# Four edits to an encoder layer's order of work: banks for row transposes, earlier weight splits and a reload, the rank of an output group, and the home of one weight block

## The chip, the cores and the metric

The kernel runs on one core of a Trainium2 chip. A core has five engines with queues of their own: PE (TensorE, matmuls and transposes), DVE (VectorE), ACT (ScalarE), POOL (GpSimd) and SP (SyncE, which here only issues DMAs). Each engine takes its instructions in the order in which the program gives them. The metric is the device time of one execution in microseconds (us); a time is the median of several runs.

## What is computed

One layer of an encoder, all in float32, on x of 1024 positions by 1024 channels. Each sub-layer stands between RMS norms and adds to x:

```python
h = rmsnorm(x, g_mix_pre);  proj = h @ w_in
y_fox = forgetting_attention(q, k, v, f_logit)        # 8 heads of 64, causal, with a decay bias
y_chk = chunked_relpos_attention(q, k, v, rel_bias)   # 8 heads of 64, own chunk and 8 before it
y = concatenate([rmsnorm(y_fox, g_fox_out), rmsnorm(y_chk, g_chk_out)])
x = x + rmsnorm(y @ w_out, g_mix_post)
h = rmsnorm(x, g_mem_pre);  mem_n = rmsnorm(mem, g_mem_kv)
x = x + rmsnorm(memory_cross_attention(h, mem_n, w_mq, w_mk, w_mv, w_mo), g_mem_post)   # 4 heads of 256, 256 memory rows
h = rmsnorm(x, g_ff_pre)
x = x + rmsnorm(square(relu(h @ w_ff1)) @ w_ff2, g_ff_post)                             # hidden 4096
```

## The kernel before

**Splits.** Every float32 operand of a large product is split into a high part (`hi`, a rounded copy made by ACT) and a low part (`lo`, the rest, a subtraction on DVE or POOL). A product is then three matmuls (`mm3`, line 191): hi by hi, hi by lo, lo by hi. So each weight block that PE uses has a load on SP, a `hi` on ACT and a `lo` behind it, and each result that PE uses again has a copy on ACT and a subtraction on DVE.

**Buffers.** Large tiles come from shared sets: `u4` (30 buffers of 128 x 1024 values), `klo` (4 buffers for the low parts of the attention keys), `w` (2 pairs for split weights), `wq` (1 pair, second stage only), `wraw` (3 for weights as loaded). Results of PE land in eight banks, two each under the names `mm`, `s`, `tr` and `pv`.

**Three stages.**

1. Projections and attention. Eight pairs of heads follow one another in the order `ORDER` (line 346). Scores (`score_steps`), transposes of the probabilities (`turn_steps`, tile `ptr`) and products with the values (`value_steps`, tile `pv`) run over heads and groups of 256 queries. What lies between them is `filler_steps` (line 1342): the projections, then `memory_steps` (line 908), which makes the memory keys (tile `mk`, 8 blocks) and the memory values (tile `mv`, 8 weight blocks named by half nh and pair kp: mv 00 to mv 13).
2. Output products `mix_steps` (tile `yw`, weights `wo`), in two groups g of heads and two halves th of positions; closing of rows; query products `query_steps` (tile `mq`); memory scores and transposes (`ms`, `mtr`); memory output products (`memory_out_steps`, tile `mo` in the `pv` banks); `product_steps` (tile `ym`).
3. The feed-forward part, in which blocks of the first product are formed with sums of blocks so that seven products do the work of eight.

**The planner.** The order within stages 1 and 2 isn't written out. `Flow` (line 56) plays the work forward on a clock of its own with a cost for each step. Each PE step is a generator's yield: a cost and a condition. `Flow.run` takes, at each point of the planned time, the first stream in its list whose condition holds, and so lays down PE's order. Work of the other engines is put into lists (`put`, `chain`, `load`) with the time from which it may start, a cost and a level; each engine takes the lowest level first, then the earliest. The costs set only this order; on the chip every instruction waits for its real inputs. `Tokens` (line 39) counts free buffers and banks in planned time: a condition such as `free["u4"].ready(4)` holds when four are free.

- `Stock` (line 367) loads and splits the weight blocks in one fixed order. `home` says where the split block goes: `w`, `wq` or two `u4` buffers. The split of a block waits until its home is free, and those behind it wait with it. `done` (line 445) gives the buffers back.
- `memory_steps` asks for four free `u4` buffers and both `mm` banks ahead of the first mv step (line 934).
- `Outputs` (line 962) reads back the attention outputs, seven `u4` buffers for each of four groups, as soon as all scores are done; `one` (line 978) makes `yT_hi`, `yT_lo` and the sum of squares `sq`, all at level 1. The sums over channels (tile `ssh`) are made by `rstd_steps`. Splits of weights stand at level 2 on ACT and level 1 on DVE.
- `close_row` (line 1076) ends a row of 128 positions: a first root (`inverse_rms`, line 1041: two small POOL instructions), the addition to x (line 1087), a square sum on ACT, a second root, and the scaled row (line 1093). The planner's cost of one root is 0.95.
- `row_steps` (line 1156) transposes the scaled rows, four at a time into one bank, for `h2T` (both halves) and `h3T` (first half): 8 groups each. Its yield wants a `tr` bank; ACT copies `hi` (line 1181), DVE subtracts `lo` (line 1178), and then the bank is free.

**The start of the feed-forward part** (lines 1721 to 1835) is written out by hand. Four units (`Turn`, line 1649) transpose the last rows (`turn`, tile `trx`), form sums of blocks with their high parts (`sums`), and make the low parts (`low`). Between them PE works through the first products of seven blocks (`ahead`, line 1626: tiles `px` and `py`, 12 matmuls each), whose weights `split_ahead` (line 1618) splits, `hi` on ACT (line 1579) and `lo` on DVE (line 1582). Their results go to memory and `reload` brings each back for the main loop. Before the change, block 3 is split behind `units[1].low()`, block 5 behind `units[3].sums()`, and the first `reload` is issued behind the load of block 1's second weights.

Of the kernel before, what the change touches and what calls it, by code (L numbers as in the profile page):

```python
# [14 lines left out]
F32 = mybir.dt.float32  # L15
# [7 lines left out]
P = 128  # L23
# [112 lines left out]
def build(ctx, tc, nc, out, t):  # L136
# [230 lines left out]
    class Stock:  # L367
# [3 lines left out]
        def __init__(self):  # L371
            self.blocks = []
            for n, (kind, pr) in enumerate(ORDER):
                if n == 5:
                    self.blocks.append("norm")
                b = (0 if kind == "f" else 8) + pr
                self.blocks.append((("q", n), t["w_qk"][b], [P, KC, P]))
                if n > 3:
                    self.blocks.append((("v", n), t["w_v"][n - 4], [P, KC, P]))
                if n == 7:  # L380
                    self.blocks.append("mem")
                self.blocks.append((("k", n), t["w_qk"][b + 4], [P, KC, P]))
# [12 lines left out]
            self.home.update({("mk", nb): "u4" for nb in range(1, KC, 2)})  # L395
            self.home.update({("mv", nh, kp): "u4" for nh in range(2) for kp in (1, 3)})
            turn = 0
            for b in self.blocks:
                if b[0][0] in ("mq", "mo"):
                    if b[0][:3] == ("mo", 1, 1):  # L400
                        self.home[b[0]] = "u4"
                    elif b[0][:2] != ("mo", 1):
                        self.home[b[0]] = ("w", "w", "wq")[turn % 3]
                        turn += 1
            self.raw, self.w, self.turned = {}, {}, 0
            self.to_load, self.to_split = list(self.blocks), []
# [9 lines left out]
        def hi(self, key):  # L416
            raw, nm = self.raw[key], "_".join(map(str, key))
            home, shape = self.home.get(key, "w"), list(raw.shape)
            if home == "w":
                w = [wp.tile(shape, F32R, tag=x, bufs=2, name=x + nm) for x in ("whi", "wlo")]  # L420
            elif home == "wq":
                w = [p2x.tile(shape, F32R, tag="wq", bufs=2, name=x + nm) for x in ("whi", "wlo")]
            else:
                w = [u4(x + nm, shape) for x in ("whi", "wlo")]
            nc.scalar.activation(w[0], raw, AF.Copy)
            self.w[key] = w
# [17 lines left out]

        def done(self, key):
            home = self.home.get(key, "w")
            for _ in range(1 + (home == "u4")):
                free[home].give(flow.end)

        def pump(self):  # L450

            while self.to_load:
                if isinstance(self.to_load[0], str):
                    n = 3 if self.to_load[0] == "norm" else 2
                    if not free["raw"].ready(n):
                        break
                    for _ in range(n):
                        free["raw"].take()
                    (mem_norm if self.to_load.pop(0) == "norm" else mem_loads)()
                    break  # L460
                if not free["raw"].ready():
                    break
                free["raw"].take()
                key = self.to_load[0][0]
                self.load()
                flow.put("D", flow.now, 0.55, lambda: None, lambda at, k=key: seen.__setitem__(("raw", k), at + 4.2))
            while self.to_split and there(("raw", self.to_split[0])):
                key = self.to_split[0]
                home = self.home.get(key, "w")
                n = 1 + (home == "u4")  # L470
                if not free[home].ready(n):
                    break
                for _ in range(n):
                    free[home].take()
                self.to_split.pop(0)
                vec = key[0] not in "qkv" and (key[0] != "mk" or key[1] % 2)
                self.turned += 1

                def halves(at, key=key, eng="V" if vec else "G"):
# [482 lines left out]
    class Outputs:  # L962
# [15 lines left out]
        def one(self, th, g):  # L978
# [3 lines left out]
            os = [u4(f"oin{th}{g}{i}", (P, 2, HT), F32) for i in range(2)]  # L982
            parts[th, g] = yh, yl, sq
            split = all_of(("y", th, g), 4)

            def summed(at):
                adds = [lambda o=o: nc.vector.tensor_add(sq, sq, o) for o in
# [4 lines left out]
                    for _ in range(2):  # L992
                        free["u4"].give(end)

                flow.chain(at, [("V", 0.7, call) for call in adds], done, 1)

            squared = all_of(("squares", th, g), 4, summed)
            for i in range(2):
                for j in range(2):
# [4 lines left out]
                    def loaded(at, gc=gc, o=o, dh=dh, dl=dl, dst=dst):  # L1004
# [2 lines left out]
                            ("V", 0.75, lambda: nc.vector.scalar_tensor_tensor(  # L1007
                                dl, o, gc, f(dh), op0=ALU.mult, op1=ALU.subtract))],
                            lambda end: (split(end), flow.put("S", end, 0.63, lambda: nc.scalar.activation(
                                dst, o, AF.Square), squared, 1)), 1)  # L1010

                    flow.load(flow.now, lambda o=o, kc=kc: nc.sync.dma_start(o, od[kc][th]), loaded, 7.0 - 3 * g)

# [62 lines left out]
    def close_row(nm, n, at, dst, gnext, then):  # L1076
# [5 lines left out]
        def root(k, a, b=None):  # L1082
            r[k] = inverse_rms(a, f"r{nm}{n}{k}", b)
# [5 lines left out]
        def store(end):  # L1089
            flow.load(end, lambda: nc.sync.dma_start(dst[n], xin[nm, n]), mark(("x1d", n)) if nm == "w" else None, 3)  # L1090
            rest = [("S", 1.1, lambda: square_sum(xin[nm, n], s2)),
                    ("G", 0.95, lambda: root(1, s2)),
                    ("V", 1.3, lambda: nc.vector.scalar_tensor_tensor(y, xin[nm, n], r[1], gains[gnext],
                                                                      op0=ALU.mult, op1=ALU.mult))]
            flow.chain(end, rest, lambda t_: (free["xt"].give(t_), then(t_)), 1)
# [5 lines left out]
            else:  # L1101
                flow.put("G", end + 0.5, 0.0, lambda: None, wait)

        flow.put("G", at, 0.95, lambda: root(0, ss[:, 0:1], ss[:, 1:2]), wait, 1)

    def mix_steps(g):

# [48 lines left out]
    def row_steps(nm, th, dst, name):  # L1156

        for a in (0, 2):
            for k in range(0, KC, 2):
                yield (0.436, lambda: there(*((dst, th * 4 + a + q) for q in range(2))) and free["tr"].ready()  # L1160
                       and ((dst, th) in acts or free["u4"].ready(8)))
                if (dst, th) not in acts:
                    for _ in range(8):
                        free["u4"].take()
                    acts[dst, th] = Act(f"{name}{th}")
                free["tr"].take()
                act, y = acts[dst, th], ys[nm, th][0]
                tr = mm_tile([P, 2, 2, P], f"tr_{name}{th}{a}{k}", "tr")
                for j in range(2):
                    for q in range(2):  # L1170
                        nc.tensor.transpose(tr[:, j, q, :], y[a + q][:, (k + j) * P:(k + j + 1) * P], ident)
# [2 lines left out]
                dh = act.h[i][:, o:o + 2, a * P:a * P + 256]  # L1174
                dl = act.l[i][:, o:o + 2, a * P:a * P + 256]

                def lo(at, src=src, dh=dh, dl=dl, key=(dst, "T", th, a, k)):
                    flow.put("V", at, 0.7, lambda: nc.vector.tensor_sub(dl, src, f(dh)),
                             lambda end: (free["tr"].give(end), seen.__setitem__(key, end)))

                flow.put("S", flow.end, 0.6, lambda src=src, dh=dh: nc.scalar.activation(dh, src, AF.Copy), lo)
        for _ in range(4):
# [570 lines left out]
    pws = [pool("pw0")]  # L1753
    pw = pws[0]
    add[1]()
    units[1].low()
    split_ahead(3, raws.pop(3))
    raws[6] = ff1_raw(6)
    add[2] = ahead(2)
    units[2].turn()  # L1760
# [5 lines left out]
    class Weights:  # L1766
# [27 lines left out]
        def split(self, n):  # L1794
# [4 lines left out]
            else:  # L1799
                self.w[n] = HiLo(raw, width, p, tag, 2, f"{n}{self.j}").both(nc.vector)  # L1800

    cur, nxt = Weights(0), Weights(1)
    cur.load(0)
    cur.load(1)
    nxt.load(0)
    add[3] = ahead(3)
    units[2].low()
    add[3]()
    units[3].turn()
    units[3].sums()  # L1810
    split_ahead(5, raws.pop(5))
    add[4] = ahead(4)
    add[4]()
    units[3].low(1)
# [1 line left out]
    nxt.load(1, True)  # L1816
    cur.sums(nc.vector)
    cur.sum4(nc.vector)
    saved = {}

    def reload(j):
        both = u4(f"p1r{j}", (P, 2, HT), F32)
        nc.sync.dma_start(both, p1d[j])
        saved[j] = both[:, 0, :], both[:, 1, :]

    reload(0)
    add[5] = ahead(5)
    cur.split("s23")
    units[3].low(2)
# [340 lines left out]
```

## Time and profile before

| | us |
|---|---|
| median of 3 runs | 1495.43 |
| lowest and highest | 1493.68, 1496.63 |
| the profiled execution | 1496.05 |
| its span, first to last instruction | 1494.3 |

The profile is of one execution. Its page gives the busy time of each engine, and further views answer questions to the trace: groups of instructions with their mean durations, waits with what ended them, instructions in order of time, and the busy time in chosen stretches with the TensorE clock that was granted. In a row of the timeline the first number is the start in us from the span's start, the second the duration, then engine, line, operation, written tile, read tiles and shape; the bracket at the end is the idle time of the engine just before it and what ended it. PE, PEld, DVE, ACT, POOL and SPq stand for matmuls, weight loads, the three other computing engines and the queue that issues DMAs.

### The profile page before, as it was taken

What the parts mean: (1) busy time and instruction counts of PE and PEld (TensorE: products, weight loads), DVE (VectorE), ACT (ScalarE), POOL (GpSimd) and SP (SyncE); (2) the same over time, 40 slices, a digit from 0 to 9 for tenths busy, and PEclk for the clock granted to TensorE, in tenths of its full rate; (3) what the DMA queues carried; (4) which work ended last, traced back from release to release, by engine and by line L of the source; (5) the groups of instructions that cost most, each with busy time, mean ns of one, the idle gap of its engine ahead of it and who ended that gap; (6) DMA issues with size and microseconds to landing.
All of it is one profiled execution on the core that took longest, in us unless ns stands there. A gap on an engine that the chain in (4) does not pass through costs nothing.

```text
span 1494.3 us, 21605 instructions
## 1 busy us (share of the span) xinstructions
PE 1471.7 (98%) x7606; PEld 1252.0 (84%) x7606; DVE 949.8 (64%) x1644; ACT 798.4 (53%) x1417; POOL 387.5 (26%) x613
## 2 busy tenths in 40 slices
PE   8999999999999999999999999999999999999998
PEld 8989888888889888888888887888888888888886
DVE  6777667566576825974374687674555665646577
ACT  6567577565577735553353455555555553443442
POOL 0144455344345200421031413333233000000021
PEclk9999999999999999999999999999999999999999
DMA  7133222422315642451241446764445695436475
GB/s 269 48 86 80 80 66 84 134 68 58 90 45 167 199 132 85 151 202 57 87 168 57 141 156 202 261 234 155 150 149 180 227 346 195 141 126 212 171 252 197
DMA packets 83485, 220.68 MB, mean 148 GB/s; under 512 B 10008, under 2 KB 14112, under 8 KB 83376
## 3 DMA queue, kind: packets, MB, share of 16 engines
q1 hardware_dynamic: 83376, 219.30, 44.5%
q8 instruction: 60, 0.98, 0.3%
q14 instruction: 49, 0.40, 0.1%
HBM read 159.96 MB, written 50.91 MB: 141 GB/s over the span
## 4 chain that ended last, share of the span: by engine, by line
PE 91%; DVE 4%; ACT 1%; DMA 1%; POOL 1%; issue 1%; SPq 0%; DVEq 0%; POOLq 0%; ACTq 0%
PE ptr L692 4%; PE fx L194 4%; PE fx L195 4%; PE fx L193 4%; PE fy L194 3%; PE fy L193 3%; PE fy L195 3%; PE px L195 3%; PE px L194 3%; PE px L193 3%; PE pv L730 2%; PE pv L729 2%; PE k L193 2%; PE k L194 2%; PE k L195 2%; PE yw L194 2%
## 5 line engine op out<-in xcount | busy, mean ns | idle before, releaser
L698 DVE TENSOR_TENSOR pl<-ptr,ph 128x512 fp32r<-128x512 f32 (+1 forms) x152 | 92.3, 616 | 39.6 <-ACT ph L701 34.6
L1894 ACT ACTIVATE whif<-ra 128x1024 fp32r<-128x1024 f32 x37 | 39.2, 1060 | 120.5 <-PE fy L194 62.6
L1896 DVE TENSOR_TENSOR wlof<-ra,whif 128x1024 fp32r<-128x1024 f32 x37 | 45.3, 1226 | 89.6 <-ACT whif L1894 89.6
L701 ACT ACTIVATE ph<-ptr 128x512 fp32r<-128x512 f32 (+1 forms) x152 | 79.3, 540 | 39.3 <-PE ptr L692 33.2
L2010 POOL TENSOR_SCALAR rf<-sf 128x1 f32<-128x1 f32 x8 | 8.2, 1027 | 326.6 <-ACT jf L1995 326.3
L730 PE MATMUL pv<-pl,vs 128*128 128x256 f32 x304 | 79.3, 285 | 1.9 <-DVE pl L698 1.9
L729 PE MATMUL pv<-ph,vs 128*128 128x256 f32 x304 | 80.1, 287 | 0.0
L193 PE MATMUL fx<-vhif,whif 128*128 128x512 f32 x168 | 65.4, 389 | 0.0
L195 PE MATMUL fx<-vhif,wlof 128*128 128x512 f32 x168 | 65.4, 389 | 0.0
L194 PE MATMUL fx<-vlof,whif 128*128 128x512 f32 x168 | 65.4, 389 | 0.0
L730 PEld LDWEIGHTS pv<-pl,vs 128*128 128x128 f32 x304 | 57.8, 190 | 6.6 <-DVE pl L698 1.5
L729 PEld LDWEIGHTS pv<-ph,vs 128*128 128x128 f32 x304 | 57.5, 189 | 4.0
L1784 POOL TENSOR_TENSOR sc<-wf,wf 128x512 f32<-128x512 f32 x14 | 21.4, 1530 | 145.4 <-DMA wf<-in_w_ff 105.9
L193 PE MATMUL k<-hT_hi,whik 128*128 128x512 f32 x128 | 52.6, 411 | 0.0
L193 PE MATMUL mq<-h2T_hi,whimq 128*128 128x512 f32 x128 | 52.1, 407 | 0.0
L193 PE MATMUL q<-hT_hi,whiq 128*128 128x512 f32 x128 | 50.9, 398 | 0.0
L194 PE MATMUL yw<-wlowo,yT_hi 128*128 128x512 f32 x128 | 49.9, 390 | 0.6 <-DVE wlowo L431 0.6
L193 PE MATMUL ym<-whimo,oT_hi 128*128 128x512 f32 x128 | 50.3, 394 | 0.1
L193 PE MATMUL yw<-whiwo,yT_hi 128*128 128x512 f32 x128 | 50.3, 393 | 0.0
L194 PE MATMUL k<-hT_lo,whik 128*128 128x512 f32 x128 | 50.2, 392 | 0.0
L195 PE MATMUL mq<-h2T_hi,wlomq 128*128 128x512 f32 x128 | 50.1, 392 | 0.0
L194 PE MATMUL q<-hT_lo,whiq 128*128 128x512 f32 x128 | 50.1, 391 | 0.0
(606 smaller groups left out, 5032.5 us busy)
## 6 DMA issues: line engine op xcount, KB each, us to landing
ra<-gd SPq DMA_DIRECT2D x56, 512.0 KB, 3.9
wg<-in_w_ff SPq DMA_DIRECT2D x56, 512.0 KB, 6.2
wf<-in_w_ff SPq DMA_DIRECT2D x38, 512.0 KB, 4.1
gd<-s SPq DMA_DIRECT2D x48, 256.0 KB, 2.1
wrawmq<-in_w_mq SPq DMA_DIRECT2D x16, 512.0 KB, 3.7
wrawmo<-in_w_mo SPq DMA_DIRECT2D x16, 512.0 KB, 3.8
gd<-u SPq DMA_DIRECT2D x32, 256.0 KB, 2.1
gd<-g SPq DMA_DIRECT2D x25, 256.0 KB, 2.4
```

The costliest lines, as they stand in the source:

```text
L193: nc.tensor.matmul(ps, lh, rh, start=start, stop=False, skip_group_check=more)
L194: nc.tensor.matmul(ps, lh, rl, start=False, stop=False, skip_group_check=more)
L195: nc.tensor.matmul(ps, ll, rh, start=False, stop=stop, skip_group_check=more)
L692: nc.tensor.transpose(tr[:, m, :], sp[:, k * P:(k + 1) * P], ident)
L698: flow.put("V", at, 0.7, lambda: nc.vector.tensor_sub(pl[:, live, :], tr[:, live, :], f(ph[:, live, :])), done)
L701: flow.put("S", flow.end, 0.6, lambda ph=ph, tr=tr, live=live: nc.scalar.activation(ph[:, live, :], tr[:, live, :], AF.Copy), split)
L729: nc.tensor.matmul(pv, v, ph[:, hs, :], start=c == 0 and half == 0, stop=False)
L730: nc.tensor.matmul(pv, v, pl[:, hs, :], start=False, stop=c + 1 == len(steps) and half == 1)
L1784: eng.tensor_sub(sc[:, k1], r0[:, k0], r1[:, k0])
L1894: nc.scalar.activation(ah, ra, AF.Copy)
L1896: nc.vector.tensor_sub(al, ra, f(ah))
L2010: nc.gpsimd.tensor_scalar(r, ssf[b][:, 0:1], ssf[b][:, 1:2], EPS, op0=ALU.add, op1=ALU.add)
```

## The change

It has six parts. The memory value block mv 01 gets its split parts from `klo` buffers instead of `u4`. The first output group's work goes from level 1 to level 3. The planner's cost of a root goes from 0.95 to 1.5 in both places of `close_row`. `row_steps` takes a `tr` bank, or a `pv` bank when no `tr` bank is free. In the feed-forward part block 3 is split ahead of `units[1].low()` and block 5 ahead of `units[3].turn()`. The first `reload` moves ahead of the load of the next block's weights.

```diff
-            self.home.update({("mv", nh, kp): "u4" for nh in range(2) for kp in (1, 3)})
+            self.home.update({('mv', 0, 1): 'klo', ('mv', 0, 3): 'u4', ('mv', 1, 1): 'u4', ('mv', 1, 3): 'u4'})
...
+            elif home == "klo":
+                w = [p1.tile(shape, F32R, tag="klo", bufs=4, name=x + nm) for x in ("whi", "wlo")]
...
-            for _ in range(1 + (home == "u4")):
+            for _ in range(1 + (home in ("u4", "klo"))):
...
-                n = 1 + (home == "u4")
+                n = 1 + (home in ("u4", "klo"))
...
+            lv = 3 if g == 0 else 1
...
-                flow.chain(at, [("V", 0.7, call) for call in adds], done, 1)
+                flow.chain(at, [("V", 0.7, call) for call in adds], done, lv)
...
-                                dst, o, AF.Square), squared, 1)), 1)
+                                dst, o, AF.Square), squared, lv)), lv)
...
-                    ("G", 0.95, lambda: root(1, s2)),
+                    ("G", 1.5, lambda: root(1, s2)),
...
-        flow.put("G", at, 0.95, lambda: root(0, ss[:, 0:1], ss[:, 1:2]), wait, 1)
+        flow.put("G", at, 1.5, lambda: root(0, ss[:, 0:1], ss[:, 1:2]), wait, 1)
...
-                yield (0.436, lambda: there(*((dst, th * 4 + a + q) for q in range(2))) and free["tr"].ready()
+                yield (0.436, lambda: there(*((dst, th * 4 + a + q) for q in range(2))) and (free["tr"].ready() or free["pv"].ready())
                        and ((dst, th) in acts or free["u4"].ready(8)))
+                bk = "tr" if free["tr"].ready() else "pv"
...
-                free["tr"].take()
+                free[bk].take()
...
-                tr = mm_tile([P, 2, 2, P], f"tr_{name}{th}{a}{k}", "tr")
+                tr = mm_tile([P, 2, 2, P], f"tr_{name}{th}{a}{k}", bk)
...
-                             lambda end: (free["tr"].give(end), seen.__setitem__(key, end)))
+                             lambda end: (free[bk].give(end), seen.__setitem__(key, end)))
...
     add[1]()
+    split_ahead(3, raws.pop(3))
     units[1].low()
-    split_ahead(3, raws.pop(3))
...
     cur.load(0)
     cur.load(1)
+    reload(0)
     nxt.load(0)
     add[3] = ahead(3)
     units[2].low()
     add[3]()
+    split_ahead(5, raws.pop(5))
     units[3].turn()
     units[3].sums()
-    split_ahead(5, raws.pop(5))
...
-    reload(0)
     add[5] = ahead(5)
```

More of the change, by code (lines that the diff above doesn't have):

```diff
@@ L1175, in row_steps, with lo @@
                 dl = act.l[i][:, o:o + 2, a * P:a * P + 256]
-                def lo(at, src=src, dh=dh, dl=dl, key=(dst, "T", th, a, k)):
+                def lo(at, src=src, dh=dh, dl=dl, key=(dst, "T", th, a, k), bk=bk):
                     flow.put("V", at, 0.7, lambda: nc.vector.tensor_sub(dl, src, f(dh)),
-                             lambda end: (free["tr"].give(end), seen.__setitem__(key, end)))
+                             lambda end: (free[bk].give(end), seen.__setitem__(key, end)))
                 flow.put("S", flow.end, 0.6, lambda src=src, dh=dh: nc.scalar.activation(dh, src, AF.Copy), lo)
@@ L1800, in split, with reload @@
                 self.w[n] = HiLo(raw, width, p, tag, 2, f"{n}{self.j}").both(nc.vector)
+    saved = {}
+    def reload(j):
+        both = u4(f"p1r{j}", (P, 2, HT), F32)
+        nc.sync.dma_start(both, p1d[j])
+        saved[j] = both[:, 0, :], both[:, 1, :]
     cur, nxt = Weights(0), Weights(1)
@@ L1818, in build @@
     cur.sum4(nc.vector)
[L1819 to L1824, printed above, removed]
-    reload(0)
     add[5] = ahead(5)
```

## The prediction

> **What bounds the kernel now.** I read the page first: its engine busy line, then the chain that ended last.
>
> ```profile
> span 1494.3 us, 21605 instructions
> PE 1471.7 (98%) x7606; PEld 1252.0 (84%) x7606; DVE 949.8 (64%) x1644; ACT 798.4 (53%) x1417; POOL 387.5 (26%) x613
> ...
> PE 91%; DVE 4%; ACT 1%; DMA 1%; POOL 1%; issue 1%; SPq 0%; DVEq 0%; POOLq 0%; ACTq 0%
> ```
>
> TensorE (PE) is the bound from end to end. The change adds and removes no matmul, so it can only close holes between matmuls: the span holds 1494.3 - 1471.7 = 22.6 us outside PE's work. The view of waits, for PE alone, says what ended the holes (columns: total, times, longest):
>
> ```profile
> PE pv L730 <- DVE pl L698: 1.9, 4, 0.9
> PE tr_h3T L1171 <- DVE ym L1093: 1.5, 1, 1.5
> PE px L195 <- DVE wlo_a L1582: 1.4, 2, 0.9
> ...
> PE tr_h2T L1171 <- DVE h2T_lo L1178: 1.2, 1, 1.2
> PE px L193 <- ACT whi_a L1579: 1.2, 1, 1.2
> ...
> PE yw L194 <- DVE wlowo L431: 0.6, 1, 0.6
> ```
>
> These six rows are where the edits are: 1.9 + 1.5 + 1.4 + 1.2 + 1.2 + 0.6 = 7.8 us. The view of stretches adds a second cost, a lower granted clock behind two of the holes (columns: stretch, its length, busy time of PE, weight loads, DVE, ACT and POOL, then PEclk):
>
> ```profile
> 506.70:510.00 3.30, 1.81 (x11) 1.41 (x11) 3.21 (x7) 3.28 (x8) 0.35 (x2) 1.00 0.61 211
> 510.10:513.40 3.30, 3.30 (x9) 2.75 (x10) 3.24 (x6) 3.25 (x7) 0.00 (x0) 0.50 0.00 0
> ...
> 755.80:759.10 3.30, 1.92 (x12) 1.75 (x13) 3.26 (x4) 1.09 (x2) 0.01 (x1) 1.00 0.75 215
> 899.20:902.50 3.30, 1.61 (x6) 0.88 (x6) 1.95 (x3) 2.74 (x4) 0.00 (x0) 1.00 0.00 0
> 902.60:905.90 3.30, 3.30 (x9) 2.55 (x8) 2.02 (x3) 0.01 (x1) 0.00 (x0) 0.50 0.68 190
> ```
>
> Where PE was idle for 3.30 - 1.81 = 1.49 us or 3.30 - 1.61 = 1.69 us of a stretch, the next 3.3 us ran at clock 0.50. The stretch at 755.8, idle for 3.30 - 1.92 = 1.38 us, is still at 1.00, and its hole belongs to the six rows. So the two emptiest stretches each cost another 3.3 / 2 = 1.65 us. All that the edits can return is therefore 7.8 + 3.3 = 11.1 us. The profiled execution took 1496.05 us (its span and 1.75 around it), which makes 1484.95 at best; the median of the three runs, 1495.43, lies 0.62 lower.
>
> **Value block in key buffers, first output group ranked last.** This is the end of attention:
>
> ```profile
> 510.08 0.55 PE L730 MATMUL pv<-pl,vs 128*128 128x256 f32 x1 [0.47 <-DVE pl L698]
> ...
> 510.86 0.63 PE L193 MATMUL mv<-whimv,mT_hi 128*128 128x512 f32 x1
> ```
>
> The last pv steps run alone, each waiting for its split. The memory value products (mv), which could fill the holes, start only when pv is over. The code says why: of 30 u4 buffers, at that point 4 hold mT, 4 km, 2 vs2, 14 the two output groups, 2 the last mk block, and 4 the blocks mv 01 and mv 03. None is left; the end of mk returns 2, mv's first step asks for 4 (line 934), and only the end of pv brings the other 2. With mv 01 in klo buffers, which the heads of ORDER's entry 6 have returned by then, 4 are free when mk ends, and mv can run between the pv steps as soon as the second mm bank is read. I count 1.5 of the 1.9 us as closed (bounds 0 and 1.9; near the full row, because only the first of the four holes may lie ahead of that bank) and the slow stretch of 1.65 with it: **3.1 us**. The gains and rows that are loaded over the klo place wait until mv 01 is used; no output product needs them before the second output group, so this costs nothing. If a load on SP were queued behind them, an output weight would come late: that is in the next bound.
>
> Ranking the output group last lets the mv and output weight splits pass yT_hi, yT_lo and the squares on ACT and DVE.
>
> ```profile
> 510.00:540.00 30.00, 29.32 (x130) 24.21 (x131) 19.53 (x26) 16.62 (x25) 3.34 (x2) 0.94 0.64 183
> ```
>
> Both engines have room there (DVE 19.53 and ACT 16.62 us busy of 30), so the delayed work hides under mv, if it ends before the output products, which now come some 3 us sooner. The hole of 0.6 there waits for an output weight's split; those splits follow the mv splits, which are now first. I take **0.3 us** gained, with bounds of 0.6 gained and 3.1 lost, the whole advance; nearer the gain, because of that room.
>
> **Row transposes in both bank pairs.** PE's row, then DVE's:
>
> ```profile
> 629.64 0.44 PE L1171 MATMUL tr_h2T<-ident,yw 128*128 128x128 f32 x2 [1.17 <-DVE h2T_lo L1178]
> ```
>
> ```profile
> 628.90 1.28 DVE L1178 TENSOR_TENSOR h2T_lo<-tr_h2T,h2T_hi 128x512 fp32r<-128x512 f32 x2
> ```
>
> Two groups fill the two tr banks, and the third waits until DVE has read the first. With pv free, all four go through at once. The query products behind them still need the first lo, near 629.6, so of the 1.17 us the two other groups fill about 2 x 0.4: **0.8 us** goes (bounds 0 and 1.2).
>
> **Root cost 1.5 instead of 0.95.** It changes the planner's order alone. What a root takes (a tensor_scalar and a tensor_tensor on POOL) is in the groups of that engine, mean ns behind the comma:
>
> ```profile
> L1047 POOL TENSOR_TENSOR rw<-rw,mhalf 128x1 f32<-128x1 f32 x16 | 11.3, 705 | 1.3
> L1046 POOL TENSOR_SCALAR rw<-ssw 128x1 f32<-128x1 f32 x8 | 6.5, 813 | 24.4 <-ACT junk L1039 24.0
> L1047 POOL TENSOR_TENSOR rm<-rm,mhalf 128x1 f32<-128x1 f32 x8 | 6.4, 802 | 0.7
> L1044 POOL TENSOR_SCALAR rw<-s2w 128x1 f32<-128x1 f32 x8 | 5.1, 636 | 17.4 <-ACT junk L1039 17.3
> ```
>
> 813 + 705 = 1.52 us and 636 + 705 = 1.34 us: the old figure is 0.4 to 0.6 short, the new one right. The h3T transposes pay for it:
>
> ```profile
> 757.18 0.98 PE L1171 MATMUL tr_h3T<-ident,ym 128*128 128x128 f32 x7 [1.48 <-DVE ym L1093]
> ```
>
> Two roots stand in each row's chain, so the plan now puts these transposes at least 2 x 0.55 = 1.1 us later, with query products ahead of them. **1.2 of 1.48 us** goes (bounds 0 and 1.48). What the new order does elsewhere between 540 and 840 no row shows. I bound it by none and by the 1.17 + 1.48 = 2.65 us that today's plan lets through there, a gain beyond those two holes being excluded because PE has no others there, and take about the middle, **1.2 us lost**.
>
> **Weight splits and the reload ahead of turned rows.** PE, DVE and ACT rows in turn:
>
> ```profile
> 887.79 0.50 PE L195 MATMUL px<-h3T_hi,wlo_a 128*128 128x512 f32 x1 [0.88 <-DVE wlo_a L1582]
> ...
> 900.57 0.50 PE L193 MATMUL px<-h3T_hi,whi_a 128*128 128x512 f32 x1 [1.16 <-ACT whi_a L1579]
> ...
> 901.83 0.50 PE L195 MATMUL px<-h3T_hi,wlo_a 128*128 128x512 f32 x1 [0.53 <-DVE wlo_a L1582]
> ```
>
> ```profile
> 884.11 0.68 DVE L1674 TENSOR_TENSOR T_lo<-T,T_hi 128x512 fp32r<-128x512 f32 x1
> ...
> 886.51 1.22 DVE L1582 TENSOR_TENSOR wlo_a<-wf,whi_a 128x1024 fp32r<-128x1024 f32 x1
> ```
>
> ```profile
> 893.22 0.58 ACT L1612 ACTIVATE p<-px 128x512 f32<-128x512 f32 x1
> ...
> 899.47 1.04 ACT L1579 ACTIVATE whi_a<-wf 128x1024 fp32r<-128x1024 f32 x1
> ```
>
> Block 3's lo stands behind four T_lo. Put first, it ends near 884.4 + 1.2 = 885.6, before px asks at 887.79 - 0.88 = 886.9: the 0.88 goes, and the four T_lo, now 1.2 us later, are read only by the main loop. Block 5's whi stands behind unit 3's sums. Put first, ACT starts it at 893.22 + 0.58 = 893.8, and DVE ends the lo near 896.8. PE asks at 900.57 - 1.16 - 0.88 = 898.5, so 1.16 + 0.53 go too, and the slow stretch with them: 2.57 + 1.65 = **4.2 us**. Late next is unit 3's chain by 1.2 us, and behind it block 6. Its whi now comes after that chain and one copy, near 901.4, its lo ends near 903.9, and PE asks for the lo about 898.5 + 24 x 0.24 + 0.5 = 904.8, with 24 matmuls of block 5 spaced 0.24 apart. That cover is 0.9 us wide; without it up to 1.2 us come back (bounds 3.0 and 4.2). The reload's one DMA moves ahead of a weight load that waits for block 6's split anyway, and its buffer comes free when unit 3 is turned: nothing.
>
> **Sum.** 3.1 + 0.3 + 0.8 + 1.2 - 1.2 + 4.2 = 8.4 us; 1496.05 - 8.4 = 1487.65, and 1487.03 by the median. I forecast 1487.3.
>
> **Rivals.**
>
> *The slow stretches stay*, or come back behind other holes: 3.3 us less gain, 1487.3 + 3.3 = 1490.6. Against it stand the rows at 510 and 902, each right behind an emptiest stretch; for it, that 1.38 us idle did nothing and 1.49 did, so that little decides. Chance 0.12. The Trainium skill ("TensorE: Matmul & The Clock Gate", Part 1) says that the clock halves after a wholly idle window of about 3.4 us, in windows that run free of the program. By that rule holes under 2 us cost no clock and the result is this rival's; this trace contradicts it, with 1.49 us idle of 3.30.
>
> *The stall moves to the first output product*: y or an output weight is late, the 3.1 us turn into a wait at yw, and such a hole halves the clock once: 1487.3 + 3.1 + 1.65 = 1492.1. Against it stands the room on ACT and DVE. Chance 0.08.
>
> *Nothing much is bought*: mv still waits for a buffer or bank, and block 6 takes block 5's place. Only 0.8 + 0.88 stay: 1495.4 - 1.7 = 1493.7. Against it stands the count of buffers. Chance 0.10.
>
> *Slower*: row transposes hold pv banks that the memory output products (mo) need. There are 24 groups of row transposes; if half of them sit in pv and each holds up mo, which PE takes in order, for 1.0 us, 12 us are lost: 1499.3. From (8.4 + 3.0) / 12 = 0.95 us a group on, the kernel is slower by over 0.2%. For it: a bank is held until DVE's lo, some 1.5 us. Against it: the planner knows both pairs and puts query products between. Chance 0.10.
>
> **How the numbers follow.** The forecast keeps 0.60, from 1484.5 to 1490. A measurement of this kernel can tell about 0.2% (3 us) from no change. Faster by more: 0.60 + 0.12 + 0.08 = 0.80; within it: 0.10; slower: 0.10. The range, 1484.5 to 1493.0, holds the forecast and the first two rivals.
>
> **What would show it.** Right: mv matmuls between the last pv steps and no clock of 0.50 behind 510; no tr_h2T wait over 0.5 us; tr_h3T not waiting for ym; no px wait on whi_a or wlo_a near 887 and 900. Wrong: mv still starting after pv; yw waiting for y or wlowo by over 1 us; px waiting for block 6; mo waiting for a bank that a row's lo reads.

## The result and the profile after

The changed kernel takes 1484.4 us (median of 6 runs, 1482.25 to 1486.49) where the kernel before, on the same chip, takes 1494.24 (6 runs, 1493.22 to 1496.63): ratio 0.9929, 95% interval 0.9919 to 0.9939, 9.8 us less. A second measurement, made with the experiments below, gave 1484.84. The profiled execution took 1484.06, 12.0 less than the profiled one of before. The forecast was 1487.3 with a range from 1484.5: the sign and the mechanisms held, and the time is 2.9 us under the forecast and 0.1 below the range. Of the 2.9 us, 1.2 come from the kernel before, which the forecast took at 1495.43 and which measured 1494.24 beside the changed one. By the medians the gain is 9.8 us, and in the profiled pair it is 12.0, where 8.4 was forecast.

The page of the changed kernel, its span and engine line:

```profile
span 1482.3 us, 21601 instructions
PE 1466.0 (99%) x7606; PEld 1250.3 (84%) x7606; DVE 948.6 (64%) x1644; ACT 797.3 (54%) x1417; POOL 391.3 (26%) x613
```

PE does the same 7606 matmuls in 5.7 us less busy time, and the span holds 16.3 us outside them instead of 22.6. More than half of the fall in busy time is the half clock that is gone (about 3.2 us, worked out below). Of the six wait rows that the prediction named, the view of waits of the changed kernel has one left, at 0.3, and a new one:

```profile
PE pz L193 <- DVE g L1948: 1.2, 1, 1.2
...
PE pv L732 <- DVE pl L700: 0.3, 1, 0.3
```

The view of stretches, of the kernel before and then of the changed one (stretch, length, busy time of PE, weight loads, DVE, ACT and POOL, then PEclk, DMA share and GB/s):

```profile
620.00:640.00 20.00, 18.83 (x92) 15.57 (x91) 19.05 (x23) 10.53 (x20) 9.55 (x13) 1.00 0.59 204
...
860.00:905.00 45.00, 42.43 (x196) 34.39 (x195) 36.03 (x50) 24.28 (x43) 6.89 (x10) 0.97 0.40 138
```

```profile
500.00:540.00 40.00, 39.70 (x215) 34.18 (x214) 29.09 (x42) 26.82 (x42) 4.96 (x10) 1.00 0.70 233
...
620.00:640.00 20.00, 20.00 (x110) 17.20 (x109) 18.85 (x24) 10.64 (x19) 8.52 (x10) 1.00 0.74 245
...
860.00:905.00 45.00, 45.00 (x212) 37.30 (x211) 41.29 (x59) 25.04 (x42) 3.42 (x6) 1.00 0.47 158
905.00:920.00 15.00, 13.77 (x61) 11.12 (x60) 7.87 (x11) 8.08 (x12) 11.50 (x8) 1.00 0.63 209
```

PE has no hole in the stretches of the edits but the 0.3 at pv, and no half clock. The new hole stands in the last stretch. PE's rows of the changed kernel at the edited places:

```profile
505.35 0.35 PE L732 MATMUL pv<-pl,vs 128*128 128x256 f32 x1 [0.30 <-DVE pl L700]
...
505.77 0.39 PE L193 MATMUL mv<-whimv,mT_hi 128*128 128x512 f32 x1
...
621.79 1.91 PE L1175 MATMUL tr_h2T<-ident,yw 128*128 128x128 f32 x16
...
751.02 1.91 PE L1175 MATMUL tr_h3T<-ident,ym 128*128 128x128 f32 x16
...
900.65 0.39 PE L193 MATMUL px<-T_hi,v0hi_s 128*128 128x512 f32 x1
...
911.08 0.39 PE L194 MATMUL pv<-T_lo,whi_s1a 128*128 128x512 f32 x1
911.31 0.39 PE L195 MATMUL pv<-T_hi,wlo_s1a 128*128 128x512 f32 x1
912.93 0.47 PE L193 MATMUL pz<-B_hi,u0hi_s 128*128 128x512 f32 x1 [1.24 <-DVE g L1948]
913.24 0.39 PE L194 MATMUL pz<-B_lo,u0hi_s 128*128 128x512 f32 x1
```

mv now starts right behind the first late pv step, and both sets of 16 row transposes go through in one piece. The kernel before reached the first matmul of the main loop, px on v0hi_s, here:

```profile
914.01 0.39 PE L193 MATMUL px<-T_hi,v0hi_s 128*128 128x512 f32 x1
```

At that point the gain is 914.01 - 900.65 = 13.4 us; the hole at pz gives 1.4 of it back.

The last four rows of the changed kernel also show how to price a hole. Matmuls follow one another 911.31 - 911.08 = 0.23 us apart, though each lasts 0.39, for they overlap. From the last one before the hole to the first behind it lie 912.93 - 911.31 = 1.62 us: the hole cost 1.62 - 0.23 = 1.39, while the idle column says 1.24. What is missing is the overlap, which has to be built up again. Worked out in the same way, the holes of the six rows of before cost 2.79 (pv), 0.75 (yw), 1.33 (tr_h2T), 1.64 (tr_h3T) and 3.07 (px), together 9.6 us instead of the 7.7 to which the idle times of these ten holes add up. (Some expectations below use 1.41 for tr_h2T; the starts of its transposes, 628.20 before the hole and 629.64 behind it, at a spacing of 0.11, give 1.33.) The first matmul behind a hole is slow as well: 913.24 - 912.93 = 0.31 us pass to the next one, 0.08 more than the usual 0.23. Over the ten holes of before this adds about 0.9 us, and behind the two holes of the changed kernel 0.15.

**The account of the profiled pair:** 9.6 - 0.55 (the pv hole that stayed) - 1.4 (pz) + 2 x 1.6 (the two half-clock stretches, in which matmuls start 0.43 us apart instead of 0.23, so that each loses about 1.6 of its 3.4 us) = 10.85 of the 12.0 us. The slow first matmuls bring it to 11.6.

The chain behind the new hole, from the timelines of the SP queue, POOL, ACT and DVE of the changed kernel:

```profile
895.49 0.33 SPq L1571 DMA_DIRECT2D wf<-in_w_ff  x1
...
898.66 0.65 SPq L1781 DMA_DIRECT2D wfu<-in_w_ff  x1
...
904.97 1.29 POOL L1788 TENSOR_TENSOR sc<-wf,wfu 128x512 f32<-128x512 f32 x1 [35.82 <-DMA p1d<-p]
...
909.03 1.06 ACT L1583 ACTIVATE v1hi_s<-sc 128x1024 fp32r<-128x1024 f32 x1 [7.28 <-POOL sc L1790]
...
910.12 1.33 DVE L1586 TENSOR_TENSOR v1lo_s<-sc,v1hi_s 128x1024 fp32r<-128x1024 f32 x1 [4.91 <-ACT v1hi_s L1583]
...
912.09 0.69 DVE L1948 TENSOR_TENSOR g<-pz,u 128x512 f32<-128x512 f32 x1
```

The profile names a store, p1d<-p, as what ended POOL's wait, but POOL's sum reads wfu, and the view of DMAs has that load's time from issue to landing:

```profile
wfu<-in_w_ff SPq DMA_DIRECT2D x1, 512.0 KB, 6.2
```

It lands at 898.66 + 6.2 = 904.86, and POOL starts at 904.97. The add that frees PE's bank (L1948) comes late by its place in DVE's order: DVE stands for 4.91 us at v1lo, which comes ahead of it. That waits for ACT, ACT for POOL's three sums, and these for the load of wfu, issued at 898.66 behind another weight load and four stores. In the kernel before the main loop began 13.4 us later and this load was issued 8.3 us later (at 906.91), so that all this was over in time.

### The profile page after: what moved, and what is told of

Read it like the earlier page. It is cut to its first block, busy times and chain, and to the rows that moved or that the text cites. A ratio compares the mean times of both kernels' runs of the same rounds, so it can differ in the third digit from the quotient of the medians.

```text
span 1482.3 us, 21601 instructions
## 1 busy us (share of the span) xinstructions
PE 1466.0 (99%) x7606; PEld 1250.3 (84%) x7606; DVE 948.6 (64%) x1644; ACT 797.3 (54%) x1417; POOL 391.3 (26%) x613
## 5 line engine op out<-in xcount | busy, mean ns | idle before, releaser
L195 PE MATMUL k<-hT_hi,wlok 128*128 128x512 f32 x128 | 50.1, 392 | 0.0
```

The lines of the kernel that those rows point to most:

```text
L195: nc.tensor.matmul(ps, ll, rh, start=False, stop=stop, skip_group_check=more)
```

## The experiments

Theory A: a hole costs its idle time and 0.15 to 0.25 us of refill, the emptiest stretches cost half-clock time besides, and the planner's new order costs nothing once all parts are in. Theory B is the prediction's own pricing. All ratios are to the kernel before, measured on the same chip. A gain in us that stands behind a ratio is that share of the median of before in the same measurement (1495.12, 1494.62 or 1495.69), not the difference of the two medians.

### The two halves of the change

ff_only is the kernel before with the feed-forward edits, stage12_only the changed kernel without them:

```diff
+    split_ahead(3, raws.pop(3))
     units[1].low()
-    split_ahead(3, raws.pop(3))
...
+    reload(0)
     nxt.load(0)
...
+    split_ahead(5, raws.pop(5))
     units[3].turn()
     units[3].sums()
-    split_ahead(5, raws.pop(5))
```

> The kernel before with the feed-forward edits alone (both weight splits and the reload moved). Theory A (a hole costs its idle time and about 0.2 us of refill behind it, emptiest stretches cost half-clock time besides, and the parts of the change add up): the px holes give back 1.05 + 1.32 + 0.70 = 3.07 us and the half-clock stretch behind them 1.7, and the product pz of block 0, which waits for the sums of the next block, costs 1.40: 3.4 us less than before, ratio 0.9977. pv (1.9), tr_h2T (1.2), tr_h3T (1.5) and yw (0.6) keep their waits, and the wait of pz at about 1.2 us is there. Theory B (the prediction's pricing): 4.2 us less, ratio 0.9972, and no wait of pz, since nothing but block 6 was named as late next. A px wait for block 6 would show the 0.9 us of cover gone.

> The changed kernel without the feed-forward edits. Theory A: the holes at pv 2.24, yw 0.76, tr_h2T 1.41, tr_h3T 1.64 and one half-clock stretch of 1.7 go in full, and the new order loses nothing between 540 and 840: 7.7 us less than before, ratio 0.9948. Theory B (the prediction's terms): 3.1 + 0.3 + 0.8 + 1.2 - 1.2 = 4.2 us less, ratio 0.9972. In both the three px rows (1.2 + 1.4) stay and the wait of pz on g does not come up; a second half-clock stretch behind px at about 892 is to be seen or not, which tells whether it belongs to that hole.

ff_only: 1491.24, ratio 0.9970 (0.9960 to 0.9981), 4.5 us less (3.9 by the medians). The interval holds both theories; the trace decides. No px row is left, and the hole at pz is there:

```profile
PE pz L193 <- DVE g L1944: 0.7, 1, 0.7
```

So the feed-forward edits cause it, as an earlier main loop meets sums that are no earlier. stage12_only: 1487.08, ratio 0.9942 (0.9927 to 0.9957), 8.7 us less (8.0 by the medians). The interval excludes B's 4.2 and holds A's 7.7. The px holes stay, and a half-clock stretch follows them, now 8 us earlier:

```profile
890.91:894.33 3.42, 1.73 (x7) 0.83 (x6) 1.72 (x3) 3.07 (x5) 0.00 (x0) 1.00 0.00 0
894.33:897.74 3.41, 3.41 (x9) 2.65 (x9) 2.02 (x4) 0.00 (x0) 0.00 (x0) 0.50 0.55 179
```

### The end of attention: buffers or ranks

klo_only and rank_only are the kernel before with one part each:

```diff
-            self.home.update({("mv", nh, kp): "u4" for nh in range(2) for kp in (1, 3)})
+            self.home.update({('mv', 0, 1): 'klo', ('mv', 0, 3): 'u4', ('mv', 1, 1): 'u4', ('mv', 1, 3): 'u4'})
```

```diff
+            lv = 3 if g == 0 else 1
...
-                                dst, o, AF.Square), squared, 1)), 1)
+                                dst, o, AF.Square), squared, lv)), lv)
```

> The kernel before with only the value block in key buffers. Theory A (u4 buffers alone hold mv back): mv runs between the last pv steps, three of the four pv rows and the half clock behind 510 go: 2.24 + 1.7 = 3.9 us less, ratio 0.9974; yw still waits about 0.6 us for its weight split, tr_h2T and tr_h3T stay. Rival C (the splits of mv stand behind yT and squares on DVE and ACT, so that the rank is needed too): mv starts as late as before, pv rows total 1.9 and the clock of 0.50 behind 510 stay: ratio 1.000.

> The kernel before with only the first output group's splits and squares ranked last. Theory A (u4 buffers alone hold mv back; the rank helps the output weight's split at most): mv starts after the last pv step as before, the four pv rows (1.9) and the half clock behind 510 stay, the yw hole of 0.6 goes: 0.3 to 0.8 us less than before, ratio 0.9996. Rival C (the rank brings mv between the pv steps): pv rows down to 0.3, no half clock there, 3.9 us less, ratio 0.9974.

klo_only: 1491.9, ratio 0.9976 (0.9966 to 0.9986), 3.6 us less. rank_only: 1493.98, ratio 0.9994 (0.9986 to 1.0003), not to be told from none. The waits of klo_only, then of rank_only:

```profile
PE yw L194 <- DVE wlowo L433: 0.9, 1, 0.9
...
PE pv L732 <- DVE pl L700: 0.3, 1, 0.3
```

```profile
PE pv L730 <- DVE pl L698: 2.1, 4, 1.1
```

The buffers alone bring mv between the pv steps, as counted from the code. The rank does nothing for pv. For yw it counts beside the value block, as the DVE rows of an output weight's low part show, first of klo_only, then of the changed kernel:

```profile
532.97 2.36 DVE L433 TENSOR_TENSOR wlowo<-wrawwo,whiwo 128x1024 fp32r<-128x1024 f32 x2 [2.93 <-ACT whiwo L427]
```

```profile
530.70 1.22 DVE L433 TENSOR_TENSOR wlowo<-wrawwo,whiwo 128x1024 fp32r<-128x1024 f32 x1
```

The third such part (the second half of the first row) ends at 535.33 with the value block alone and at 531.92 with both. With the rank alone it ends at 538.16, no earlier than the 538.05 of the kernel before, so the missing yw row of rank_only shows little: in the six traces without the rank the hole at yw was anything from 0.1 to 0.9 us. None of the eight traces with the rank has it. One part makes the gain, the other keeps the earlier output products from waiting. Rival C falls.

### The row transposes: banks, root cost, both

banks_only and root_only are the kernel before with one part each (the first diff shows the condition, with a cut in its lines, the second one of the two places):

```diff
-                yield (0.436, lambda: ... and free["tr"].ready()
+                yield (0.436, lambda: ... and (free["tr"].ready() or free["pv"].ready())
```

```diff
-                    ("G", 0.95, lambda: root(1, s2)),
+                    ("G", 1.5, lambda: root(1, s2)),
```

> The kernel before with only the row transposes allowed in both bank pairs. Theory A (the whole hole and its refill go, the planner's new order costs nothing): no tr_h2T row, 1.41 us less, ratio 0.9991. Theory B (the prediction's term): 0.8 us less and a tr_h2T or query product wait of about 0.4 us. Rival E (the prediction's slower case): products wait for banks that a row's lo still reads, up to 12 us more, ratio up to 1.008, with waits of mo or mq on h2T_lo or h3T_lo of about 1 us each.

> The kernel before with only the planner's root cost at 1.5. Theory A: no tr_h3T row, no new PE wait between 540 and 840, 1.64 us less, ratio 0.9989. Theory B (the prediction's terms): tr_h3T down to about 0.3 us and 1.2 us lost in new waits elsewhere between 540 and 840, together nothing, ratio 1.000.

banks_only: 1492.84, ratio 0.9986 (0.9977 to 0.9994), 2.1 us less. PE's row shows all 16 transposes in one piece, with no wait:

```profile
627.18 1.91 PE L1172 MATMUL tr_h2T<-ident,yw 128*128 128x128 f32 x16
```

No wait of mo or mq of the size of rival E comes up. root_only: 1492.94, ratio 0.9991 (0.9982 to 1.0000), hardly to be told from none. tr_h3T is gone, but the wait at tr_h2T has grown, and a half-clock stretch follows it (its waits, then its stretches):

```profile
PE tr_h2T L1171 <- DVE h2T_lo L1178: 2.0, 1, 2.0
```

```profile
629.07:632.48 3.41, 1.45 (x12) 1.04 (x11) 3.11 (x6) 1.87 (x5) 0.94 (x2) 1.00 0.64 214
632.48:635.89 3.41, 3.41 (x13) 2.92 (x12) 2.14 (x3) 1.07 (x2) 0.00 (x0) 0.50 0.35 136
```

So the prediction's fear had a ground: by itself the new plan does lose time elsewhere, in this trace 0.8 us of wait and 1.6 of half clock, more than the 1.64 that it gains. The trace is of the slowest of the twelve runs (1496.25); by the median the part alone loses nothing, and whether the half clock comes in the other runs is not shown. A's "no new wait" is wrong for this part alone. But the loss lies in the row that the other edit closes. root_banks puts the two together:

> The kernel before with two parts, the root cost of 1.5 and the row transposes in both bank pairs. Alone, the banks gave 0.9986 with no tr_h2T row, and the root cost gave 0.9991 with tr_h3T gone but tr_h2T grown from 1.2 to 2.0 us and a half-clock stretch behind it. Theory A (the loss by the new plan lies wholly in the hole at tr_h2T, which the second bank pair closes whatever its length): neither row, no stretch of 0.50 behind 632, 1.41 + 1.64 = 3.05 us less than before, ratio 0.9980. Theory B (the new plan's loss of about 1.2 us stays): a wait of 0.7 us or more at tr_h2T or at the query products, ratio 0.9988.

root_banks: 1490.23, ratio 0.9970 (0.9959 to 0.9981), 5.5 us less by the medians and 4.5 by the ratio; the interval excludes B's 0.9988. Its waits have neither tr row. By the traces the root cost is worth 1.64 - 0.8 = 0.8 us alone, less where a half clock follows, and its whole 1.64 us beside the second bank pair: these two don't simply add up. The times agree with this but don't settle it, since the interval of root_only holds both values.

### The hole at pz: an earlier load, or sums on an empty engine

early_second issues the late load first; sums_dve computes the three sums on DVE, in the 4.9 us in which it waits; after_again is the changed kernel, measured with it:

```diff
     reload(0)
+    nxt.load(1, True)
     nxt.load(0)
...
-    nxt.load(1, True)
```

```diff
-            if more:
+            if more and j:
                 nxt.sums()
                 nxt.sum4()
...
                 nc.vector.tensor_add(u2, x, p1)
+                if j == 0:
+                    nxt.sums(nc.vector)
+                    nxt.sum4()
```

> The changed kernel with one more edit: the load of the next block's second weight (wfu) is issued right behind the reload of block 0, ahead of the next block's first weight. Theory A (the 1.24 us hole at pz comes from that load, which is issued at 898.66, lands 6.3 us later and holds up the sums on GpSimd, v1hi and v1lo, behind which the g add stands): the load lands before 897, the sums start with it, the pz row goes, 1.40 us less than the changed kernel, ratio 0.9920 against before where the changed kernel had 0.9929. Rival D (the add waits for DVE's queue, not for the load): the pz row stays at about 1.2 us, ratio as the changed kernel.

> The changed kernel itself once more, as the measure for the two kernels built on it. All theories: ratio 0.993 with its interval over the first one's (0.9919 to 0.9939), a wait of pz on g of about 1.2 us, no clock of 0.50 between 20 and 1479.

> The changed kernel with one edit: the three sums for block 1 go to DVE, behind the first u add at 904.53, where DVE waits 4.9 us in the changed kernel; GpSimd keeps the fourth. Theory A (the hole at pz hangs on those sums, done by GpSimd in 1.34 us each from 904.97, with DVE empty meanwhile): DVE takes three of 0.72 from 905.2 to 907.4, v1hi and v1lo follow by 909.8, the g add ends near 911, before PE asks at 911.7: the pz row goes, nothing collides since GpSimd has only the fourth sum left, 1.40 us less than the changed kernel (ratio 0.001 lower). Theory G (as with the earlier load, the stall only moves, for DVE is the engine that is late): waits of px or pz on DVE of 1 us or more remain, no gain.

early_second: 1486.31, ratio 0.9936 (0.9923 to 0.9949), no gain on the changed kernel with its 0.9929 and 0.9935. The pz row on g is gone, but others stand in its place:

```profile
PE px L193 <- DVE u L1929: 0.9, 1, 0.9
...
PE pz L195 <- DVE wlo_s1a L1586: 0.5, 1, 0.5
```

The load did come early; the first weight's load was then the later of the two, and the sums began at 900.42 instead of 904.97. There they ran beside DVE. Its rows, then POOL's:

```profile
900.10 0.68 DVE L1678 TENSOR_TENSOR T_lo<-xf,T_hi 128x512 fp32r<-128x512 f32 x1
900.70 1.78 DVE L1678 TENSOR_TENSOR T_lo<-c,T_hi 128x512 fp32r<-128x512 f32 x1
902.41 0.68 DVE L1618 TENSOR_TENSOR g<-py,p 128x512 f32<-128x512 f32 x1
903.01 1.71 DVE L1586 TENSOR_TENSOR wlo_s1a<-wf,whi_s1a 128x1024 fp32r<-128x1024 f32 x1
```

```profile
900.42 1.52 POOL L1788 TENSOR_TENSOR sc<-wf,wfu 128x512 f32<-128x512 f32 x1 [30.95 <-DMA wf<-in_w_ff]
902.02 1.62 POOL L1789 TENSOR_TENSOR wfu<-wfu 128x512 f32<-128x512 f32 x1
903.72 2.15 POOL L1790 TENSOR_TENSOR sc<-wfu,wf 128x512 f32<-128x512 f32 x1
```

The subtraction T_lo takes 0.69 us while POOL is empty (in the changed kernel, at 902.73) and 1.78 beside a sum on POOL; the sum takes 1.29 alone (rows of the changed kernel) and up to 2.15. The add g at 902.41, which reads a result of PE, keeps 0.68 though a sum runs beside it. The Trainium skill (GPSIMD Engine Reference, 1. Specifications) says that GpSimd shares its SBUF interfaces with VectorE and contends with DVE instructions that have two inputs in SBUF; these rows agree: T_lo and wlo have two, while the g add has one of its inputs in PE's banks. So neither D nor A was right: the load was the cause, and removing it put the sums where they slow the engine that is late.

sums_dve: 1484.24, ratio 0.9927 (0.9914 to 0.9941), beside 1484.84 and 0.9935 (0.9922 to 0.9948) of after_again. The difference of 0.6 us is not separated from none; the trace shows the step. The DVE rows:

```profile
907.44 0.68 DVE L1929 TENSOR_TENSOR u<-px,p1r 128x512 f32<-128x512 f32 x1
908.04 0.68 DVE L1788 TENSOR_TENSOR sc<-wf,wfu 128x512 f32<-128x512 f32 x1
...
911.30 1.39 DVE L1586 TENSOR_TENSOR v1lo_s<-sc,v1hi_s 128x1024 fp32r<-128x1024 f32 x1 [1.13 <-ACT v1hi_s L1583]
...
913.32 0.69 DVE L1951 TENSOR_TENSOR g<-pz,u 128x512 f32<-128x512 f32 x1
```

The add ends at 914.01 and PE comes to pz at 914.42: no wait. In this run a wait of 0.4 came up at another place, where px asks for block 6's low part (in early_second it was 0.1, and in the changed kernel none). after_again shows why the gain is small too: its pz wait was 0.8, not 1.2, for how late the load is against PE varies from run to run.

### A longer hole, for the clock

The first sum for block 1 is computed a second time, or a second and a third, into the same place, which makes v1 later (hole_512 shown; hole_two repeats it twice):

```diff
             eng.tensor_sub(sc[:, k1], r0[:, k0], r1[:, k0])
+            if j == 1:
+                eng.tensor_sub(sc[:, HT:HT + 512], r0[:, 0:512], r1[:, 0:512])
```

> The changed kernel with the first of GpSimd's three 128x512 sums for block 1 computed twice, so that the wait of pz at 911.69 grows from 1.24 by one such sum, 1.37 us a step, to about 2.6 us. Theory A (PE idle for more than about 1.5 us of one 3.4 us window halves the clock of the next window): a stretch of 0.50 behind about 914, 1.4 + 1.7 = 3.1 us more than the changed kernel, ratio 0.9950 where that had 0.9929; if a window's border cuts the hole into parts under 1.5 us, no stretch. Theory F (only the empty time counts, no clock): 1.4 us more, ratio 0.9938, clock 1.00 throughout. The Trainium skill (TensorE: Matmul & The Clock Gate, Part 1) is on F's side, since it names a wholly idle window of about 3.4 us.

> The changed kernel with the first of GpSimd's sums for block 1 computed three times, as a larger dose than before, where one repeat left the hole at 1.41 us since the load landed earlier and PE came later. Now 1.41 + 1.37 = 2.8 us of wait of pz. Theory A (PE idle for more than 1.5 us within one 3.41 us window of a fixed grid halves the clock of the next one): unless the grid cuts the hole into parts under 1.5 us, a stretch of 0.50 behind it, about 1.6 + 1.7 = 3.3 us more than the changed kernel, ratio 0.002 higher. Theory F (only a wholly idle window counts): 1.6 us more, ratio 0.001 higher, and clock 1.00 to 1479.

hole_512 (one repeat): 1486.55, ratio 0.9947 (0.9934 to 0.9959). The load landed earlier and PE came later, so the hole was 1.41 instead of 2.6, and the run tells nothing of the clock. hole_two (two repeats): 1489.47, ratio 0.9962 (0.9948 to 0.9975), 4.6 us above after_again by the medians. Its hole was 3.8 us, and its stretches along the windows of the clock are:

```profile
911.79:915.21 3.42, 0.85 (x4) 0.38 (x2) 1.57 (x2) 2.00 (x2) 2.12 (x3) 1.00 0.00 1
915.21:918.62 3.41, 2.20 (x5) 1.82 (x6) 3.25 (x5) 2.28 (x4) 3.29 (x2) 0.50 0.05 13
918.62:922.03 3.41, 3.41 (x9) 2.64 (x8) 0.62 (x2) 0.70 (x2) 2.88 (x2) 0.50 0.98 309
```

Idle for 3.42 - 0.85 = 2.57 us of a window, PE got half the clock in the next, as theory A has it. In that one it was idle for another 1.21, and the half clock stayed for one more, which A had not foreseen. F falls, and with it the rule as the Trainium skill states it (TensorE: Matmul & The Clock Gate, Part 1), half clock after an idle window of about 3.4 us, if a wholly idle one is meant: no window was wholly idle here. Its windows of that length that run free of the program, though, are what these rows show.

## Why the forecast was right in kind and short in size

By the prediction's own steps, with what each measured:

- **What bounds the kernel now.** Right: PE was the bound, and the six rows held the gain. Wrong: "All that the edits can return is therefore 7.8 + 3.3 = 11.1 us", and the 1484.95 "at best" from it. The idle column leaves out 0.16 to 0.25 us of refill a hole, 1.9 us over the ten holes; with it the holes and the two half-clock stretches held 9.6 + 3.2 = 12.8 us. The low end of the range, 1484.5, lies close to that bound (by the median of before the bound is 1484.3).
- **Value block in key buffers.** The count of buffers was right, and klo_only shows it. "I count 1.5 of the 1.9 us as closed" was too little: three of the four holes closed, at 2.24 us with refill; the fourth, 0.55, lies ahead of mv.
- **First output group ranked last.** 0.3 forecast, 0.75 measured, by the hole that is gone in the profiled pair; its size varies from run to run (above). The cover on ACT and DVE held.
- **Row transposes in both bank pairs.** 0.8 forecast, 1.33 measured: nothing was left behind the transposes, and no product waited for a bank.
- **Root cost 1.5.** 1.2 forecast, 1.64 measured. The step that failed most is the next one, "What the new order does elsewhere between 540 and 840 ... take about the middle, **1.2 us lost**". In the full change the loss is nothing: PE has no wait there above 0.1. root_only and root_banks show why. The loss exists, but in the tr_h2T row, which the second bank pair closes. For the two parts together the prediction had 0.8 + 1.2 - 1.2 = 0.8 us; root_banks has 1.33 + 1.64 = 3.0 by its trace and an interval of 2.8 to 6.1.
- **Weight splits and the reload.** 4.2 forecast; by the trace 3.07 + 1.6 - 1.4 = 3.3, and 4.5 (2.8 to 6.0) for ff_only. "Late next is unit 3's chain ... and behind it block 6" was incomplete: late next was the main loop's own supply, POOL's sums for block 1. The cover of block 6 was not the 0.9 us of the prediction but about nothing: it was late by 0.1 and 0.4 in two runs and in time in the other traces with these edits.
- **The slow stretches.** Two of 1.65 forecast as gone, two gone. That was partly luck: whether a hole costs one depends on how it falls into the windows (below).

The terms that were too small, 0.7 + 0.5 + 0.5 + 0.4 + 1.2 + 0.5 = 3.8, less the 1.4 at pz that had not been seen, make 2.4 of the 3.6 us by which the 12.0 of the profiled pair exceed the 8.4 of the forecast; the slow first matmuls behind the holes make another 0.8. By the medians the gain exceeds it by 1.4 us. That the time came out below the range, by 0.1, hangs on the 1.2 us by which the kernel before measured lower, and so on chance, while the step that was wrong shows in the traces. None of the rivals came true. All four signs that were to show the steps right are there.

## What to carry to other kernels

Price a hole in a pipelined engine from the start of the last instruction before it to the start of the first behind it, less the usual spacing, and not by its idle time alone; where the first one behind is slow too, go on to the second, less two spacings. When two edits touch one plan, ask whether the loss of the one lies in the wait that the other removes, before a loss is deducted. When a stage becomes earlier by 13 us, look for the first load in the next stage whose issue does not come earlier with it; and before work is moved into a gap of its engine, see what the engine that shares memory with it does at that time.

## What the runs showed of the hardware

**The clock.** The granted clock changes on a grid of 3.41 us. In the fourteen traces, behind the first 17 us and away from the end, a window at full clock was followed by half clock when PE had been idle for 1.53 us of it or more (1.53, 1.61, 1.65, 1.65, 1.69, 1.69, 1.87, 1.88, 1.96, 2.57) and never at 1.51 or less. The same hole therefore costs 1.6 us more or nothing more. The three px holes of before stand in seven traces; the half clock came in three of them and not in four, where the grid cut them. Two of those, klo_only (the 1.51, with the window behind it) and rank_only (1.16), along the grid:

```profile
896.95:900.36 3.41, 1.90 (x7) 1.30 (x8) 2.45 (x4) 2.35 (x3) 0.00 (x0) 1.00 0.05 10
900.36:903.77 3.41, 3.41 (x17) 2.81 (x16) 2.08 (x3) 0.60 (x1) 0.00 (x0) 1.00 0.79 238
```

```profile
897.26:900.67 3.41, 2.25 (x10) 1.52 (x9) 1.71 (x4) 3.23 (x6) 0.00 (x0) 1.00 0.00 0
```

At the start of the program that border does not hold. These are two windows of the kernel before:

```profile
4.86:8.27 3.41, 1.67 (x15) 1.43 (x13) 1.42 (x2) 2.34 (x3) 0.00 (x0) 1.00 0.85 303
8.27:11.69 3.42, 1.97 (x14) 1.77 (x15) 2.22 (x4) 2.84 (x5) 0.00 (x0) 1.00 1.02 414
```

PE was idle for 3.41 - 1.67 = 1.74 us of the first, and the next is at full clock. Five of the fourteen traces have such a window there, with 1.61 to 1.84 us of idle, while in stage12_only 1.74 us was followed by half clock. So PE's idle time in the profile alone does not decide it, and what else does is open.

**The start.** In nine of the fourteen traces one or two such stretches stand in the first 17 us, where PE waits for its first weight; neither trace of the pair before and after has one. At 1.6 us each they may be much of the spread of 4.2 us between runs of the changed kernel, whose mean clock was 0.999 at 1482.25 us and 0.996 at 1486.49. That is argued from those two numbers; no run was made for it.

**DVE beside POOL.** A DVE subtraction with both inputs in SBUF took 1.78 instead of 0.69 us while POOL summed, and POOL's sum up to 2.15 instead of 1.29.
